# Seven block products for eight in three quarters of an MLP down-projection, with the block sums on GpSimd

## The chip, the core and the metric

The kernel runs on one core of one Trainium2 chip. The metric is the device time of one execution in microseconds (us). Timed are whole executions; beside them one execution was recorded by the hardware profiler, and all durations of single instructions come from that one.

## What is computed

The reference is one decoder block on 512 tokens of width 1024, all in float32. Two token mixers (a state-space branch and a gated delta rule) run side by side, are merged by gates and projected by w_out; an MLP follows. Only the part behind the mixers is touched in earnest:

```
x = x + g1 * rmsnorm(merged @ w_out, norm_mix_post)
h = rmsnorm(x, norm_mlp_pre) * (1.0 + sc2) + sh2
y = square(relu(h @ w_mlp_up)) @ w_mlp_down
x = x + g2 * rmsnorm(y, norm_mlp_post)
```

h is 512 x 1024, w_mlp_up is 1024 x 4096, w_mlp_down is 4096 x 1024. The up-projection and the down-projection are of the same size.

## The kernel before

Matmuls take float32 operands in the type fp32r, which keeps fewer bits. To keep accuracy every operand is split in two: a high half (the value cast to fp32r) and a low half (the value less its high half). `mm3` (line 149) then makes three matmuls of a pair of tiles: high by high, low by high, high by low. A weight tile of 128 x 1024 goes through `dense_w` (line 140): SyncE issues its load into a tile `raw`, ScalarE casts it to `whi` (line 145), VectorE subtracts to get `wlo` (line 146). Each of the three tags has three buffers, so weight n can't be split before the matmuls of weight n-3 are done.

The mixers (up to about line 1237) run in an order written out by hand. Behind them the instructions of each engine are put in order by a planner of the framework at build time, which goes by the program's order as its priority and by planned durations; each engine then runs its own list strictly in that order. GpSimd (POOL in the profile), VectorE (DVE), ScalarE (ACT), TensorE (PE) and SyncE's DMA queue (SP) each have such a list.

After the mixers come the branch projections, then w_out with the norms (lines 1271 to 1356). `norms` adds the residual into the tiles `x1`, which stay in SBUF to the end of the kernel, as do the two rows `gates`. `up_part` (line 1289) starts the first three hidden blocks of the MLP early.

The MLP (lines 1359 to 1438) goes over four quarters q of the 4096 hidden channels. In a quarter, eight hidden blocks m of 128 channels are made: 24 matmuls of 512 columns (8 slices of the contraction by 3), then on ScalarE a ReLU (line 1375) and a square (line 1378), which is the high half at once, and on VectorE the exact square (line 1377) and the low half (line 1379). The block is kept as `act`, 128 channels x 512 tokens, in two halves. 16 buffers of `act` allow a quarter's blocks to be made beside the last quarter's use of theirs. Then follow two halves hf of the 1024 output columns. For each, four banks of PSUM (one for each 128 tokens) collect over four weight tiles kp, each of which holds two slices of 128 hidden channels by 512 columns. In `down` (line 1382) a weight tile serves 4 token blocks x 2 slices x 3 = 24 matmuls; a quarter has 8 weight tiles and 192 matmuls. The banks are then added to the sums `ya` (copied by ScalarE, line 1408, in the first quarter; added by VectorE, line 1410, in the next ones). The last quarter ends with the last norm, the gate and the residual (lines 1413 to 1438), whose GpSimd multiply (line 1416) is the only work that GpSimd has in the MLP before its last microseconds.

[...]

Of the kernel before, what the change touches and what calls it, by code (L numbers as in the profile page):

```python
# [116 lines left out]
def hybrid_block(ctx: ExitStack, tc: tile.TileContext, x, cols, drow, rows, w_ada, w_ch, w_z,  # L117
# [284 lines left out]
    tok1 = const.tile([P, NC, P], F32, name="tok1")  # L402
    tok2 = const.tile([P, NC, P], F32, name="tok2")
    neg = const.tile([P, NC, 16], F32, name="neg")
    elast = const.tile([P, H, NC], F32, name="elast")
# [10 lines left out]
    eye = const.tile([P, 8, 32], F32, name="eye")  # L416
# [854 lines left out]
    lp = ctx.enter_context(tc.tile_pool(name="lp", bufs=1))  # L1271
    gates = []
    for n in range(2):
        g = fin.tile([P, D], F32, name=f"gate{n}")
# [5 lines left out]
        gates.append(g)  # L1280
    x1, xn = [], []
    for t in range(NC):
        xx = fin.tile([P, D], F32, name=f"x1{t}")
        nc.sync.dma_start(out=xx, in_=x[t * P:(t + 1) * P, :])
        x1.append(xx)
# [17 lines left out]
    def norms(half):  # L1303
# [5 lines left out]
        for t in tt:  # L1309
            xx = lp.tile([P, D], F32, tag="act", name="xn", bufs=16)  # L1310
            for i in range(2):
                hs = slice(i * T, (i + 1) * T)
                ve.scalar_tensor_tensor(out=xx[:, hs], in0=pp[t, i], scalar=r1[:, t % 2:t % 2 + 1],  # L1313
                                        in1=gates[0][:, hs], op0=MUL, op1=MUL)
# [44 lines left out]
    ya = [lp.tile([P, D], F32, name=f"ya{t}") for t in range(NC)]  # L1359
    sq = [lp.tile([P, 1], F32, name=f"sqn{t}") for t in range(NC)]  # L1360
    for q in range(4):
        act = []
        for m in range(8):
            mm = q * 8 + m
            if mm < len(ups):
                ps = ups[mm][1]
            else:
                w = dense_w(w_mu[mm])
                ps = lpsum()
                for k in range(KD):  # L1370
                    ks = slice(k * P, (k + 1) * P)
                    mm3(ps, (w[0][:, ks], w[1][:, ks]), h2[k], k == 0, k == KD - 1)
            a = lp.tile([P, 2, T], F32R, tag="act", name="act", bufs=16)
            rl = lp.tile([P, T], F32, tag="rl", name="rl", bufs=2)
            sc.activation(rl, ps, AF.Relu)
            s = lp.tile([P, T], F32, tag="cv", name="sq", bufs=3)
            ve.scalar_tensor_tensor(out=s, in0=ps, scalar=0.0, in1=rl, op0=MAX, op1=MUL)
            sc.activation(a[:, 0, :], rl, AF.Square)
            ve.tensor_sub(out=a[:, 1, :], in0=s, in1=a[:, 0, :].bitcast(F32))
            act.append(a)  # L1380

        def down(ps, t, w, kp, a=0, b=T):
            ts = slice(t * P, (t + 1) * P)
            for k in range(2):
                kk = 2 * kp + k
                mm3(ps[:, a:b], (act[kk][:, 0, ts], act[kk][:, 1, ts]),
                    (w[0][:, k * T + a:k * T + b], w[1][:, k * T + a:k * T + b]), kk == 0, kk == 7)
        for hf in range(2):
            hs = slice(hf * T, (hf + 1) * T)
            end = q == 3 and hf == 1  # L1390
            pp = [lpsum() for _ in range(NC)]
            if end:
                extra = [lp.tile([P, 2, T], F32R, tag="act", name="wx", bufs=16).rearrange("p a b -> p (a b)")
                         for _ in range(2)]
                ws = [dense_w(w_md[q, hf, kp], extra if kp == 3 else None) for kp in range(4)]
                pp.append(lpsum())
                for n, (a, b) in enumerate(((0, T), (0, T), (0, T), (0, 256), (256, T))):
                    for kp in range(4):
                        down(pp[n], min(n, 3), ws[kp], kp, a, b)
            else:  # L1400
                for kp in range(4):
                    w = dense_w(w_md[q, hf, kp])
                    for t in range(NC):
                        down(pp[t], t, w, kp)
            for t in range(NC):
                y = ya[t][:, hs]
                if q == 0:
                    sc.copy(y, pp[t])
                elif not end:
                    ve.tensor_add(out=y, in0=pp[t], in1=y)  # L1410
                if q < 3:
                    continue
                if hf == 0:
                    sc.activation(junk[:, 0:T], y, AF.Square, accum_out=sq[t])  # L1414
                    ve.tensor_scalar(out=sq[t], in0=sq[t], scalar1=1.0 / D, scalar2=EPS, op0=MUL, op1=ADD)
                    gp.tensor_tensor(out=y, in0=y, in1=gates[1][:, hs], op=MUL)  # L1416
                    continue

                s1 = sq[t]
                for a, b in ((0, 256), (256, T)) if t == NC - 1 else ((0, T),):  # L1420
                    ve.tensor_add(out=y[:, a:b], in0=pp[t + (a > 0)][:, a:b], in1=y[:, a:b])
                    sh = lp.tile([P, 1], F32, tag="sh", name="sh", bufs=2)
                    sc.activation(junk[:, a:b], y[:, a:b], AF.Square, accum_out=sh)
                    sn = lp.tile([P, 1], F32, tag="s1", name="s1", bufs=2)
                    ve.scalar_tensor_tensor(out=sn, in0=sh, scalar=1.0 / D, in1=s1, op0=MUL, op1=ADD)
                    s1 = sn
                    if b == T:
                        gp.tensor_tensor(out=s1, in0=s1, in1=mhalf[:, 0:1], op=POW)
                    ve.tensor_mul(out=y[:, a:b], in0=y[:, a:b], in1=gates[1][:, T + a:T + b])
                ob = lp.tile([P, D], F32, tag="ob", name="ob", bufs=2)  # L1430
                for a, b in ((0, 256), (256, 640), (640, D)) if t == NC - 1 else ((0, T), (T, D)):
                    if b == 256:
                        sc.mul(ob[:, a:b], ya[t][:, a:b], s1)
                        gp.tensor_tensor(out=ob[:, a:b], in0=ob[:, a:b], in1=x1[t][:, a:b], op=ADD)
                    else:
                        ve.scalar_tensor_tensor(out=ob[:, a:b], in0=ya[t][:, a:b], scalar=s1, in1=x1[t][:, a:b],
                                                op0=MUL, op1=ADD)
# [87 lines left out]
```

## Time and profile before

| | |
|---|---|
| time, median of 3 runs | 1483.94 us (1483.15 to 1485.08) |
| the profiled execution's own time | 1484.77 us |
| its span, first to last instruction of the program | 1483.1 us |
| PE busy | 1458.1 us (98%), 8592 matmuls |
| DVE busy | 862.5 us (58%) |
| ACT busy | 732.6 us (49%) |
| POOL busy | 370.2 us (25%) |
| granted TensorE clock | 0.996 of full speed |

A row of the profile names the source line, the engine, the operation, the tile written and the tiles read, the shapes, and then times. A line can be that of a helper: all matmuls of `mm3` are on lines 150 to 152. Matmuls overlap in the pipeline, so the time of one is not its price in a stream: the price is the distance from one start to the next. Idle time stands in brackets behind an instruction, with what ended it. The granted clock is the share of its full clock that TensorE had.

### The profile page before, as it was taken

How to read it: one execution, taken by the hardware profiler on the slowest of the kernel's cores; microseconds unless marked ns; L12 is line 12 of the kernel's file. 1: busy time of each engine (PE TensorE's matmuls, PEld its weight loads, DVE VectorE, ACT ScalarE, POOL GpSimd, SP SyncE). 2: the span in 40 equal slices, each digit the busy share in tenths (PEclk: the TensorE clock that was granted, in tenths of full speed). 3: DMA queues.
4: the chain of work that ended last, by engine and by line, in shares of the span. 5: the costliest groups of instructions: out<-in, count | busy, mean ns of one | idle time of the engine just before them, and what ended most of it. 6: DMA issues, size and time to landing. Idle time of an engine off the chain costs nothing. (4 is left out here: it accounts for less than half of the span.)

```text
span 1483.1 us, 22692 instructions
## 1 busy us (share of the span) xinstructions
PE 1458.1 (98%) x8592; PEld 1241.0 (84%) x8592; DVE 862.5 (58%) x1522; ACT 732.6 (49%) x1379; POOL 370.2 (25%) x691
## 2 busy tenths in 40 slices
PE   9999999999999999999999899999999999999998
PEld 7788898879989889888888788888878888888886
DVE  3565577677767777676777634444477324343444
ACT  6575545673764747645665635333355333132232
POOL 3005444341814607336623410000011000000002
PEclk9999999999999999999999999999999999999999
DMA  9323434543434524344343449543372233223221
GB/s 360 127 97 118 150 103 125 128 137 97 151 119 138 158 81 151 121 116 138 116 137 119 158 170 331 175 156 127 110 239 88 97 100 100 89 96 99 93 95 69
DMA packets 87070, 199.47 MB, mean 134 GB/s; under 512 B 32504, under 2 KB 33024, under 8 KB 86960
## 3 DMA queue, kind: packets, MB, share of 16 engines
q1 hardware_dynamic: 86960, 198.01, 41.3%
q8 instruction: 68, 1.11, 0.3%
q14 instruction: 42, 0.34, 0.1%
HBM read 181.10 MB, written 16.88 MB: 133 GB/s over the span
## 5 line engine op out<-in xcount | busy, mean ns | idle before, releaser
L150 PE MATMUL ps<-hT,whi 128*128 128x512 f32 x688 | 285.7, 415 | 4.8 <-ACT whi L469 4.3
L151 PE MATMUL ps<-hT,wlo 128*128 128x512 f32 x688 | 269.8, 392 | 1.2 <-DVE wlo L471 1.2
L152 PE MATMUL ps<-hT,whi 128*128 128x512 f32 x688 | 269.9, 392 | 0.0
L146 DVE TENSOR_TENSOR wlo<-raw,whi 128x1024 fp32r<-128x1024 f32 x114 | 140.0, 1229 | 199.7 <-ACT whi L145 199.7
L145 ACT CAST whi<-raw 128x1024 fp32r<-128x1024 f32 x114 | 119.4, 1048 | 210.1 <-PE pl L151 61.9
L150 PE MATMUL ps<-whi,hT 128*128 128x256 f32 (+1 forms) x536 | 166.3, 310 | 2.2 <-ACT y L715 1.4
L471 DVE TENSOR_TENSOR wlo<-raw,whi 128x1024 fp32r<-128x1024 f32 x103 | 128.1, 1244 | 64.2 <-ACT whi L469 60.3
L150 PEld LDWEIGHTS ps<-hT,whi 128*128 128x128 f32 x688 | 129.9, 189 | 31.9 <-ACT whi L469 4.5
L152 PE MATMUL ps<-wlo,hT 128*128 128x256 f32 (+1 forms) x536 | 154.3, 288 | 0.6 <-DVE wlo L471 0.6
L151 PE MATMUL ps<-whi,hT 128*128 128x256 f32 (+1 forms) x536 | 153.8, 287 | 0.0
L152 PEld LDWEIGHTS ps<-hT,whi 128*128 128x128 f32 x688 | 129.7, 189 | 28.3
L151 PEld LDWEIGHTS ps<-hT,wlo 128*128 128x128 f32 x688 | 130.1, 189 | 25.8 <-DVE wlo L471 2.4
L469 ACT CAST whi<-raw 128x1024 fp32r<-128x1024 f32 x103 | 107.3, 1044 | 67.4 <-PE ps L152 47.1
L533 DVE SCALAR_TENSOR_TENSOR cv<-ps,col,cv 128x511 f32<-128x511 f32 (+1 forms) x180 | 133.0, 742 | 8.0 <-ACT cv L527 5.4
L150 PEld LDWEIGHTS ps<-whi,hT 128*128 128x128 f32 x536 | 102.1, 190 | 5.8 <-ACT y L715 1.6
L825 POOL TENSOR_TENSOR tm<-Ub,Nb 128x60 f32<-128x60 f32 (+24 forms) x248 | 93.7, 378 | 52.5 <-DMA Nb<-btd 37.6
L151 PEld LDWEIGHTS ps<-whi,hT 128*128 128x128 f32 x536 | 102.1, 190 | 2.2
L152 PEld LDWEIGHTS ps<-wlo,hT 128*128 128x128 f32 x536 | 101.8, 190 | 2.0 <-DVE wlo L471 0.8
L827 POOL TENSOR_TENSOR Ub<-Ub,tm 128x60 f32<-128x60 f32 (+24 forms) x248 | 95.0, 383 | 19.4
L1416 POOL TENSOR_TENSOR ya<-ya,gate 128x512 f32<-128x512 f32 x4 | 5.8, 1466 | 324.8 <-ACT junk L1414 324.8
L150 PE MATMUL pl<-hT,whi 128*128 128x512 f32 (+1 forms) x184 | 66.6, 363 | 1.0 <-DVE hT L195 1.0
L151 PE MATMUL pl<-hT,wlo 128*128 128x512 f32 (+1 forms) x184 | 66.1, 362 | 0.4 <-DVE wlo L146 0.4
(502 smaller groups left out, 3049.0 us busy)
## 6 DMA issues: line engine op xcount, KB each, us to landing
raw<-in_w_ch SPq DMA_DIRECT2D x81, 512.0 KB
raw<-in_w_ada SPq DMA_DIRECT2D x48, 512.0 KB
raw<-in_w_z SPq DMA_DIRECT2D x32, 512.0 KB
raw<-in_w_up SPq DMA_DIRECT2D x32, 512.0 KB
raw<-in_w_mu SPq DMA_DIRECT2D x32, 512.0 KB
raw<-in_w_md SPq DMA_DIRECT2D x32, 512.0 KB
dc<-acd SPq DMA_DIRECT2D x16, 512.0 KB
ydr<-y SPq DMA_DIRECT2D x32, 256.0 KB
```

The lines of the kernel that those rows point to most:

```text
L145: sc.copy(hi, raw)
L146: ve.tensor_sub(out=lo, in0=raw, in1=hi.bitcast(F32))
L150: pe.matmul(ps, lhsT=lhs[0], rhs=rhs[0], start=first, stop=False)
L151: pe.matmul(ps, lhsT=lhs[1], rhs=rhs[0], start=False, stop=False)
L152: pe.matmul(ps, lhsT=lhs[0], rhs=rhs[1], start=False, stop=last)
L469: sc.copy(hi, raw)
L471: ve.tensor_sub(out=lo, in0=raw, in1=hi.bitcast(F32))
L533: ve.scalar_tensor_tensor(out=t[:, s:], in0=ps[:, :T - s], scalar=col[:, o + k:o + k + 1], in1=t[:, s:], op0=MUL, op1=ADD)
L825: gp.tensor_tensor(out=t3, in0=Ub[:, 0:r, j:j + 1].to_broadcast([P, r, n]), in1=Nb[:, j:j + 1, j + 1:32].to_broadcast([P, r, n]), op=MUL)
L827: gp.tensor_tensor(out=Ub[:, 0:r, j + 1:32], in0=Ub[:, 0:r, j + 1:32], in1=t3, op=SUB)
L1416: gp.tensor_tensor(out=y, in0=y, in1=gates[1][:, hs], op=MUL)
```

## The change

In quarters 0 to 2 the down-projection is made by a scheme of seven block products (Strassen's, in Winograd's form). The tokens are halved (256 each), the output columns are halved (512 each) and the hidden slices are taken in pairs (k0, k1), so that each pair of hidden slices gives a two-by-two block product: four activation blocks of 128 x 256 and four weight blocks of 128 x 512. In place of eight block products, seven are made, of sums and differences of blocks. The function `down7` does a quarter:

- For each pair kp it loads both weight tiles of the pair (both column halves), forms two weight differences on GpSimd, makes two hidden blocks (`hidden`), squares them into one float32 tile `pr` of four blocks, and forms the activation sums on GpSimd.
- `unit` splits two activation blocks (128 x 512 in all, or one of 128 x 256) in high and low halves, `wide` does the same to weight blocks: the cast on ScalarE, the subtraction on VectorE or GpSimd, as the caller says.
- `stage` goes over the four pairs kp with one split weight tile, one split activation tile and one or two block products of two token blocks each (`product`: three matmuls of 512 columns). The first three stages make two of the seven products each, 48 matmuls in a stage, and the fourth makes one, 24 matmuls.
- The second stage's weight tile is, once it is split, overwritten by GpSimd with the two weight differences of the third stage.
- Banks that belong to more than one output block are added to `ya` and then go on collecting (`add`, and start=False).

Quarter 3 is computed as before. To make room, `x1` is written to DRAM in `norms` and read back before the last half, `gates[0]` lives in a pool that is closed before the MLP, some tiles of the mixers move to the mixers' own pool, and `act` has 8 buffers, shared with the units. The last quarter's tiles take the tags of those pools.

The core of the diff:

```
...
+            nc.sync.dma_start(out=x1d[t], in_=x1[t])
...
+    def halves(src, dst, en):
+        sc.copy(dst[0], src)
+        en.tensor_tensor(out=dst[1], in0=src, in1=dst[0].bitcast(F32), op=SUB)
+        return dst
+    def unit(src, n, en):
+        u = mp.tile([P, 2, n, 256], F32R, tag="act", name="unit", bufs=8)
+        return halves(src, (u[:, 0], u[:, 1]), en)
+    def wide(src, en=None):
+        n = src.shape[1]
+        return halves(src, [wp.tile([P, 2, T], F32R, tag=tag, name=tag)[:, 0:n] for tag in ("whi", "wlo")], en or ve)
+    def product(ps, u, ub, w, wb, tt, first, last):
+        ts = slice(tt * P, (tt + 1) * P)
+        for n, (i, j) in enumerate(((0, 0), (1, 0), (0, 1))):
+            pe.matmul(ps, lhsT=u[i][:, ub, ts], rhs=w[j][:, wb], start=first and n == 0, stop=last and n == 2,
+                      skip_group_check=True)
+    def down7(q):
+        raw, tb, pr, s12, u1 = {}, [], [], [], []
+        for kp in range(4):
+            for hf in range(2):
+                raw[hf, kp] = mp.tile([P, 2, T], F32, tag="wr", name="wr", bufs=8)
+                nc.sync.dma_start(out=raw[hf, kp].rearrange("p a b -> p (a b)"), in_=w_md[q, hf, kp])
+            b1, b2 = raw[0, kp], raw[1, kp]
+            t = mp.tile([P, 2, T], F32, tag="tt", name="tt", bufs=4)
+            gp.tensor_tensor(out=t[:, 0], in0=b2[:, 0], in1=b1[:, 0], op=SUB)
+            gp.tensor_tensor(out=t[:, 1], in0=b2[:, 1], in1=t[:, 0], op=SUB)
+            tb.append(t)
+            a = mp.tile([P, 4, 256], F32, tag="pr", name="pr", bufs=4)
+            for k in range(2):
+                _, rl = hidden(q * 8 + 2 * kp + k)
+                sc.activation(a[:, 2 * k:2 * k + 2].rearrange("p a b -> p (a b)"), rl, AF.Square)
+            pr.append(a)
+            sm = mp.tile([P, 2, 256], F32, tag="s12", name="s12", bufs=4)
+            gp.tensor_tensor(out=sm[:, 0], in0=a[:, 1], in1=a[:, 3], op=ADD)
+            gp.tensor_tensor(out=sm[:, 1], in0=sm[:, 0], in1=a[:, 0], op=SUB)
+            gp.tensor_tensor(out=a[:, 1], in0=a[:, 0], in1=a[:, 1], op=SUB)
+            s12.append(sm)
+            u1.append(unit(a[:, 0:4:2], 2, ve))
+            gp.tensor_tensor(out=a[:, 2], in0=a[:, 2], in1=sm[:, 1], op=SUB)
...
+        def stage(us, ws, plan, after=None):
+            for kp in range(4):
+                w = ws(kp)
+                u = us(kp)
+                for ps, ub, wb, start in plan if kp < 3 else plan[::-1] if len(plan) > 1 and after else plan:
+                    for tt in range(2):
+                        product(ps[tt], u, ub, w, wb, tt, start and kp == 0, kp == 3)
+        banks = lambda: [lpsum() for _ in range(2)]
+        pa, pc = banks(), banks()
+        stage(lambda kp: u1[kp], lambda kp: wide(raw[0, kp]), [(pa, 0, 0, True), (pc, 1, 1, True)])
+        for tt in range(2):
+            add(tt, 0, pa[tt], True)
+            add(tt, 0, pc[tt])
+        pb_ = banks()
+        def w2(kp):
+            w = wide(tb[kp])
+            gp.tensor_tensor(out=tb[kp][:, 0], in0=raw[0, kp][:, 1], in1=tb[kp][:, 1], op=SUB)
+            gp.tensor_tensor(out=tb[kp][:, 1], in0=raw[1, kp][:, 1], in1=raw[1, kp][:, 0], op=SUB)
+            return w
+        stage(lambda kp: unit(s12[kp], 2, ve), w2, [(pb_, 0, 0, True), (pa, 1, 1, False)], True)
+        for tt in range(2):
+            add(tt, 1, pa[tt], True)
+        for tt in range(2):
+            add(tt + 2, 1, pb_[tt], True)
+        pc = banks()
+        stage(lambda kp: unit(pr[kp][:, 1:4:2], 2, gp), lambda kp: wide(tb[kp]), [(pc, 1, 0, True), (pa, 0, 1, False)], True)
+        for tt in range(2):
+            add(tt + 2, 1, pa[tt])
+            add(tt + 2, 0, pa[tt], True)
+        for tt in range(2):
+            add(tt + 2, 0, pc[tt])
+        stage(lambda kp: unit(pr[kp][:, 2:3], 1, gp), lambda kp: wide(raw[1, kp][:, 1:2], gp), [(pb_, 0, 0, False)])
+        for tt in range(2):
+            add(tt, 1, pb_[tt])
...
+    x1 = [mp.tile([P, D], F32, tag="tt", name="x1r", bufs=4) for _ in range(NC)]
+    for t in range(NC):
+        nc.sync.dma_start(out=x1[t], in_=x1d[t])
...
```

More of the change, by code (lines that the diff above doesn't have):

```diff
@@ L401, in hybrid_block @@
     H = 48
[L402 to L405, printed above, removed]
+    tok1 = sp.tile([P, NC, P], F32, name="tok1", bufs=1)
+    tok2 = sp.tile([P, NC, P], F32, name="tok2", bufs=1)
+    neg = sp.tile([P, NC, 16], F32, name="neg", bufs=1)
+    elast = sp.tile([P, H, NC], F32, name="elast", bufs=1)
     nA = const.tile([H, 1], F32, name="nA")
@@ L415, in hybrid_block @@
         gp.memset(tl, 0.0)
-    eye = const.tile([P, 8, 32], F32, name="eye")
+    eye = sp.tile([P, 8, 32], F32, name="eye", bufs=1)
     gp.memset(eye, 0.0)
@@ L1268, in hybrid_block @@
     up.close()
[L1271 to L1274, printed above, removed]
+    x1d = dram.tile([NC, P, D], F32, name="x1d")
+    gate1 = fin.tile([P, D], F32, name="gate1")
+    norm_scope = ExitStack()
+    lp = norm_scope.enter_context(tc.tile_pool(name="lp", bufs=1))
+    gate0 = lp.tile([P, D], F32, name="gate0")
+    for n, g in enumerate((gate0, gate1)):
         nc.sync.dma_start(out=g, in_=adr[n].partition_broadcast(P))
@@ L1309, in norms @@
         for t in tt:
-            xx = lp.tile([P, D], F32, tag="act", name="xn", bufs=16)
+            xx = lp.tile([P, D], F32, tag="xn", name="xn", bufs=4)
             for i in range(2):
@@ L1356, in hybrid_block @@
             up_part(m, slice(half * 256, (half + 1) * 256))
[L1359 to L1366, printed above, removed]
-            else:
[L1368 to L1400, printed above, removed]
-                for kp in range(4):
[L1402 to L1437, printed above, removed]
-                    nc.sync.dma_start(out=out[t * P:(t + 1) * P, a:b], in_=ob[:, a:b])
@@ new lines, in hybrid_block, with hidden @@
+    norm_scope.close()
+    mp = ctx.enter_context(tc.tile_pool(name="mp", bufs=1))
+    ya = [mp.tile([P, D], F32, name=f"ya{t}") for t in range(NC)]
+    sq = [mp.tile([P, 1], F32, name=f"sqn{t}") for t in range(NC)]
+    def hidden(mm):
+        if mm < len(ups):
+            ps = ups[mm][1]
+        else:
+            w = dense_w(w_mu[mm])
+            ps = lpsum()
+            for k in range(KD):
+                ks = slice(k * P, (k + 1) * P)
+                mm3(ps, (w[0][:, ks], w[1][:, ks]), h2[k], k == 0, k == KD - 1)
+        rl = mp.tile([P, T], F32, tag="rl", name="rl", bufs=2)
+        sc.activation(rl, ps, AF.Relu)
+        return ps, rl
@@ new lines, in down7, with add @@
+    def down7(q):
[21 more added lines that the diff above has]
+            gp.tensor_tensor(out=a[:, 2], in0=a[:, 2], in1=sm[:, 1], op=SUB)
+        def add(tt, hf, ps, first=False):
+            y = ya[tt][:, hf * T:(hf + 1) * T]
+            if first and q == 0:
+                sc.copy(y, ps)
+            else:
+                ve.tensor_add(out=y, in0=ps, in1=y)
+        def stage(us, ws, plan, after=None):
[32 more added lines that the diff above has]
+            add(tt, 1, pb_[tt])
@@ new lines, in hybrid_block, with down @@
+    for q in range(3):
+        down7(q)
+    act = []
+    for m in range(8):
+        ps, rl = hidden(24 + m)
+        a = mp.tile([P, 2, T], F32R, tag="act", name="act", bufs=8)
+        s = mp.tile([P, T], F32, tag="pr", name="sq", bufs=4)
+        ve.scalar_tensor_tensor(out=s, in0=ps, scalar=0.0, in1=rl, op0=MAX, op1=MUL)
+        sc.activation(a[:, 0, :], rl, AF.Square)
+        ve.tensor_sub(out=a[:, 1, :], in0=s, in1=a[:, 0, :].bitcast(F32))
+        act.append(a)
+    def down(ps, t, w, kp, a=0, b=T):
+        ts = slice(t * P, (t + 1) * P)
+        for k in range(2):
+            kk = 2 * kp + k
+            mm3(ps[:, a:b], (act[kk][:, 0, ts], act[kk][:, 1, ts]),
+                (w[0][:, k * T + a:k * T + b], w[1][:, k * T + a:k * T + b]), kk == 0, kk == 7)
```

47 lines of the change are left out of this document (44 added, 3 removed).

## The prediction

> **What bounds the kernel now.** I read the page's busy times first, then two stretches of the MLP in the table of busy time by stretch, then PE's timeline inside a down-projection.
>
> ```profile
> PE 1458.1 (98%) x8592; PEld 1241.0 (84%) x8592; DVE 862.5 (58%) x1522; ACT 732.6 (49%) x1379; POOL 370.2 (25%) x691
> ```
>
> ```profile
> 1210.60:1254.80 44.20, 44.20 (x196) 36.57 (x195) 18.86 (x22) 15.98 (x23) 0.00 (x0) 1.00 0.29 95
> 1254.80:1299.40 44.60, 44.60 (x194) 36.15 (x193) 15.76 (x17) 9.57 (x11) 0.00 (x0) 1.00 0.29 96
> ```
>
> The two rows are quarter 1: eight hidden blocks, then 192 down matmuls. After start, end and length the columns are PE, PEld, DVE, ACT and POOL busy, the granted clock, and the DMA share. PE is busy for all of both stretches at full clock, DVE for 16 to 19 of 44 us, ACT for 10 to 16, POOL not at all, DMA at 29%. So only fewer matmuls can shorten the MLP, and each other engine has room, on average, for work that replaces them.
>
> ```profile
> 1166.47 0.40 PE L150 MATMUL pl<-whi,act 128*128 128x512 f32 x1
> ...
> 1175.31 0.39 PE L152 MATMUL pl<-wlo,act 128*128 128x512 f32 x1
> ```
>
> These are the 1st and the 39th matmul (13 triples) of quarter 0's down-projection: 8.84 us for 38 steps, 0.2326 us from start to start. That is the price of a matmul in a stream; the 0.39 of one row is its length in the pipeline.
>
> **What is removed.** A quarter's down-projection goes from 192 to 168 matmuls (48 + 48 + 48 + 24) of the same shape: 24 x 0.2326 = 5.58 us, and 16.7 us for three quarters. The seven-product stretch needs 168 x 0.2326 = 39.1 us of PE: its stages end at 11.2, 22.3, 33.5 and 39.1 us from its start. The MLP's up-projection and quarter 3 keep their matmuls.
>
> **What is added, by engine.** The prices:
>
> ```profile
> L145 ACT CAST whi<-raw 128x1024 fp32r<-128x1024 f32 x114 | 119.4, 1048 | 210.1 <-PE pl L151 61.9
> ```
>
> ```profile
> L1378 ACT ACTIVATE act<-rl x32: 628/629/641, 1136.2 to 1432.6; 128x512 fp32r<-128x512 f32 x32
> L146 DVE TENSOR_TENSOR wlo<-raw,whi x114: 1208/1226/1661, 865.0 to 1454.3; 128x1024 fp32r<-128x1024 f32 x114
> L1379 DVE TENSOR_TENSOR act<-sq,act x32: 684/685/686, 1137.5 to 1433.9; 128x512 fp32r<-128x512 f32 x32
> L1410 DVE TENSOR_TENSOR ya<-pl,ya x14: 681/688/692, 1273.6 to 1453.5; 128x512 f32<-128x512 f32 x14
> L1416 POOL TENSOR_TENSOR ya<-ya,gate x4: 1289/1380/1812, 1451.4 to 1456.8; 128x512 f32<-128x512 f32 x4
> L1156 POOL TENSOR_TENSOR xk<-xk,zs x32: 733/744/1721, 228.1 to 870.7; 128x256 f32<-128x256 f32 x32
> ```
>
> The first is a row of the page's groups (busy us, mean ns, then idle time before). In the others the three figures behind a count are least, median and greatest duration in ns. For POOL I take the least, 1.29 us for 512 columns and 0.73 for 256, as the time of one that waited for nothing.
>
> ACT, in the seven-product stretch: at most 12 full weight casts (12.6 us), 4 half ones and 12 unit casts at 0.63 or less (10.1), so about 23 of 39 us. It stays beside PE. Nothing is booked; were ACT late by one cast, that would be 1.05 us.
>
> DVE: 12 full weight subtractions (14.7 us) in place of 8, 4 unit ones for the second stage (2.7), and 16 additions from PSUM (11.0) in place of 8: 28.4 of 39.1 us. By itself it fits too.
>
> POOL, in a whole quarter: 24 operations on 512 columns (two weight differences before and two after the second stage's split, a unit's and a weight's low half, for each of 4 pairs) and 20 on 256 (four block sums and one unit's low half): 24 x 1.29 + 20 x 0.73 = 45.6 us; PE has for it the eight hidden blocks and the stretch:
>
> ```profile
> 1216.76 0.60 ACT L1375 ACTIVATE rl<-pl 128x512 f32<-128x512 f32 x1 [4.15 <-PE pl L152]
> ...
> 1254.84 0.60 ACT L1375 ACTIVATE rl<-ps 128x512 f32<-128x512 f32 x1 [3.38 <-PE ps L152]
> ```
>
> These are the first and the eighth ReLU of quarter 1, each set off by the last matmul of its hidden block: 38.08 us for 7 blocks, 5.44 us for one, 43.5 us for eight. With the 39.1 that is 82.6 us, so POOL fits as well. But POOL and DVE do not run beside each other freely:
>
> ```profile
> 1453.28 1.30 POOL L1416 TENSOR_TENSOR ya<-ya,gate 128x512 f32<-128x512 f32 x1 [0.40 <-ACT junk L1414]
> 1455.01 1.81 POOL L1416 TENSOR_TENSOR ya<-ya,gate 128x512 f32<-128x512 f32 x1 [0.42 <-ACT junk L1414]
> ```
>
> ```profile
> 1453.48 0.69 DVE L1410 TENSOR_TENSOR ya<-pl,ya 128x512 f32<-128x512 f32 x1
> 1454.34 1.32 DVE L146 TENSOR_TENSOR wlo<-raw,whi 128x1024 fp32r<-128x1024 f32 x1 [0.17 <-ACT whi L145]
> ```
>
> The addition from PSUM (L1410) ran inside the first POOL operation at its usual 0.69. The weight subtraction (L146, both inputs in SBUF) started 0.24 us before that POOL operation ended, at 1454.58, and ended at 1455.66, that is 1.08 after it. The second POOL operation started inside the subtraction and ended at 1456.82, 1.16 after it. So a POOL operation and a DVE subtraction with two SBUF inputs take turns; the one that waits then needs 0.13 to 0.15 us less than alone, as its start is already behind it. I call what they take turns at the shared port, and its holds 1.08 (weight, DVE) and 1.15 (512 columns, POOL), and by the same 0.14 less than alone 0.55 (unit, DVE) and 0.59 (256 columns, POOL). The second pair is an estimate from the rows above.
>
> [...]
>
> **The port's bill.** Over a quarter: DVE 20 x 1.08 + 8 x 0.55 = 26.0, POOL 24 x 1.15 + 20 x 0.59 = 39.4, together 65.4 of 82.6 us. It fits. Over the seven-product stretch it does not. A split weight can be made only when the weight three before it is done, so at the stretch's start two of its weights are ready and the third's buffer comes free just then. What must then pass the port before PE can go on with the next quarter:
>
> - DVE: ten weight subtractions (the third to the twelfth weight), 10.8; the last pair's two units, 1.1; the next quarter's first hidden weight, 1.1. Sum 13.0.
> - POOL: the last pair's four block sums, 2.4; eight weight differences, 9.2; the third stage's units, 4.6; the fourth stage's units, 2.4; its weights, 4.6; and the next quarter's first weight differences for two pairs, which can be queued between these, 4.6. Sum 27.8.
>
> 40.8 us of port, and the port has nothing of this until the last hidden block's ReLU and square are through, some 1.2 us (twice 0.6). 42.0 less 39.1 is 2.9; I book a stall of 3.0 us a quarter. Ends: without the next quarter's differences it is 37.4, under 39.1, so no stall; with full durations in place of the holds it is 8.6 (the second rival). I take the middle since the handover rows give the holds, and POOL would otherwise be idle when those differences come up. The stall should sit in the third and fourth stages: the first begins with two weights ready, each weight's buffer is free 5.6 us ahead, and the late ones are the third stage's last weights, which need POOL's differences first.
>
> **Waits that come with it.** A DVE subtraction that waits for POOL holds up what is queued behind it: additions from PSUM. Banks `pa` go on collecting after an addition, so PE waits for it at the second and third stage; the first six matmuls of these stages go to another bank (1.4 us), and the stage before them ends with the other product (1.4 us more): 2.8 us of cover for two additions, 1.4 us, and a wait of 1.15. Booked at nothing; uncovered it would be about 1 us a time.
>
> The hidden blocks lose the exact square and the low half on DVE (16 operations of about 0.69 a quarter) and gain POOL's sums and a unit; the first unit of the last pair is due 8.4 us after the last hidden matmul, and ReLU, square, three sums, cast and subtraction are 0.6 + 0.6 + 3 x 0.73 + 0.6 + 0.7 = 4.7. Nothing.
>
> `x1` to DRAM and back:
>
> ```profile
> GB/s 360 127 97 118 150 103 125 128 137 97 151 119 138 158 81 151 121 116 138 116 137 119 158 170 331 175 156 127 110 239 88 97 100 100 89 96 99 93 95 69
> 1105.49 20.02 SPq L142 DMA_DIRECT2D raw<-in_w_mu  x6
> ```
>
> At the best slice's 360 GB/s a tile of 0.52 MB is 1.5 us. The reads have all of quarter 3's hidden blocks to land, 43 us. The stores stand in SP's queue among the w_out and w_mu loads, and wait there for the residual's addition with loads behind them; those loads are issued many us ahead (the six at 1105.49 go out over 20 us). Between 0 and one tile's 1.5 us I take 0.5, nearer to nothing. The tiles moved between pools, quarter 3's eight `act` buffers (free before its first square, 5.4 us into its first block) and the end cost nothing; a conflict there would show as a PE wait of a us or so at 1134 or 1454.
>
> **The sum.** 1484.8 (the profiled execution) - 16.7 + 3 x 3.0 + 0.5 = 1477.6. That execution lies 0.8 above the median of the runs, so 1476.8 for a median.
>
> **Rivals.**
>
> *PE stays the bound.* POOL's work for the next quarter keeps out of the stretch, the port has 37.4 us of claims and PE 39.1. For it: over the quarter the port has 17 us to spare, and each claim may slip by several us until it is due. Against: 37.4 leaves room for hardly one turn lost. 1484.8 - 16.7 + 0.3 - 0.8 = 1467.6.
>
> *The port becomes the bound.* Place: the seven-product stretch, third and fourth stage. Price at durations of one that waits for nothing: DVE 11 x 1.23 + 2 x 0.69 = 14.9, POOL 20 x 1.29 + 8 x 0.73 = 31.6, with 1.2 of start 47.7 us against 39.1: 8.6 us a quarter, 3.0 more than the matmuls saved. 1484.8 - 16.7 + 25.8 + 0.5 - 0.8 = 1493.6. It decides from a stall of 5.58 us a quarter on. For it: in-order lists laid out without turns lose time between turns. Against: the handover rows are shorter than full durations. [...]
>
> *DVE's queue gives it all back.* In the second stage DVE has 4 weight subtractions (4.9), 4 additions (2.8) and up to 4 waits of 1.15: 12.3 against 11.2 us, and the same at the fourth, so 2.2 more a quarter: 1484.8 - 16.7 + 15.6 + 0.5 - 0.8 = 1483.4, no change. Against: two weights of lead.
>
> That the seven products need more matmuls than counted is excluded by the loops.
>
> **How the numbers follow.** A measurement of this kernel tells about 0.2%, 3 us, from no change. Forecast (stall of 1.5 to 4.5 us a quarter, 1472 to 1481): 0.45. PE the bound: 0.25. DVE's queue: 0.1. The port: 0.2. Faster is the first two, 0.7; the same 0.1; slower 0.2. The range for 8 in 10 goes from just under the PE case to a little over the no-change case: 1466.5 to 1488; it leaves out most of the port's case.
>
> **What would show it.** In the profile after: 72 matmuls fewer, PE at 0.2326 a step within the stages. PE idle time with DVE weight or unit subtractions (or POOL low halves) as releasers, in quarters 0 to 2 alone, near 9 us in sum; POOL operations on 512 columns from 1.29 up to 2.4 us, DVE's weight subtraction up to 2.4, the additions still 0.69. No PE idle time there would show the port's bill wrong; idle time behind loads, or in the hidden blocks, would show the place wrong. The prediction fails if stalls exceed 5 us a quarter.

## The result and the profile after

The changed kernel takes 1509.57 us (median of 4 runs, 1504.29 to 1512.37) against 1484.51 of the kernel before (4 runs, 1483.15 to 1485.6). The ratio is 1.0165, with an interval of 1.0135 to 1.0195. The change makes the kernel slower by some 25 us; the prediction was 1476.8, faster by 8, and the time lies outside its range. The profiled execution took 1508.65 us with a span of 1506.9, so 23.8 us more than the span before. The accounts below are made against these two spans.

The page's busy times and granted clock of the kernel after:

```profile
PE 1453.5 (96%) x8520; PEld 1231.7 (82%) x8520; DVE 906.2 (60%) x1534; ACT 774.9 (51%) x1451; POOL 543.9 (36%) x823
...
PEclk9999999999999999999999999999989989999999
```

There are 72 matmuls fewer, as counted, but PE is busy for only 4.6 us less, and in two of the 40 slices, those that begin at 1092 and at 1206 us, its clock reads 8 tenths instead of 9 or more. The table of busy time by stretch shows where. Here are the down-projections of quarters 0 and 2 before (that of quarter 1 stands in the prediction, 44.60 us), and those of quarters 0 to 2 after, in the columns told there:

```profile
1166.20:1210.60 44.40, 44.40 (x192) 36.00 (x192) 11.10 (x10) 13.42 (x17) 0.00 (x0) 1.00 0.30 100
...
1343.30:1388.00 44.70, 44.70 (x194) 36.26 (x193) 16.12 (x18) 9.72 (x11) 0.00 (x0) 1.00 0.29 95
```

```profile
1176.10:1228.60 52.50, 43.95 (x170) 33.58 (x169) 28.22 (x24) 25.82 (x40) 43.44 (x30) 0.92 0.22 74
1272.90:1324.60 51.70, 42.75 (x169) 33.00 (x168) 35.54 (x32) 21.93 (x32) 42.83 (x30) 0.94 0.22 77
1368.70:1411.10 42.40, 39.72 (x169) 31.40 (x168) 34.38 (x31) 21.79 (x31) 35.56 (x24) 1.00 0.15 50
```

The stretches hold 168 matmuls instead of 192, and yet the first two are 8.1 and 7.1 us longer than before; the third, which no seven-product quarter follows, is 2.3 us shorter. In sum they take 146.6 us where the kernel before takes 133.7, 12.9 us more. A second loss lies ahead of the MLP. The same matmul, one that waits 1.0 us for a transposed block and starts the last part of the early hidden blocks, in PE's timeline before and after:

```profile
1121.65 0.39 PE L150 MATMUL pl<-hT,whi 128*128 128x256 f32 x1 [0.99 <-DVE hT L195]
```

```profile
1131.26 0.39 PE L150 MATMUL pl<-hT,whi 128*128 128x256 f32 x1 [1.00 <-DVE hT L195]
```

It comes 9.6 us later. 12.9 and 9.6 are 22.5 of the 23.8 us; the other 1.3 lies in the hidden blocks (0.6) and in quarter 3 and the end (0.7), by the same table's stretches, and was not followed. The list of PE's waits from the w_out stage to the end of quarter 2 (waited for: us in total, times, longest) shows both places:

```profile
PE pl L1398 <- POOL wlo L1382: 11.1, 4, 3.3
PE pl L150 <- ACT whi L145: 7.4, 1, 7.4
PE pl L1398 <- DVE wlo L1382: 4.4, 5, 1.1
PE pl L1398 <- DVE ya L1432: 3.5, 2, 1.8
PE ps L1398 <- DVE wlo L1382: 1.2, 1, 1.2
```

Line 1398 is the matmul of the seven products, line 1382 the subtraction that makes a low half, on DVE or on POOL, and line 1432 the addition of a bank to `ya`. The largest row is POOL's low halves of weights, of which the fourth stage has four a quarter. The second is not in the seven products at all: a weight of w_out that is late once by 7.4 us. Around it the granted clock is at half:

```profile
1090.20:1100.40 10.20, 4.96 (x11) 3.48 (x12) 4.90 (x4) 3.42 (x4) 0.00 (x0) 0.50 0.73 265
```

PE works for 4.96 us of it, at half pace; that is some 2.3 us more (an estimate from PE's timeline: the 11 matmuls from 1095.40 to 1100.24 start 0.44 us apart in place of 0.2326), and with the 7.4 it makes up the 9.6. Two theories were formed from this, one for each place.

**Fourth stage: the order of POOL's list.** POOL's timeline at the end of quarter 0, and PE's beside it:

```profile
1208.93 1.30 POOL L1411 TENSOR_TENSOR tt<-wr 128x512 f32<-128x512 f32 x1
1210.31 2.15 POOL L1412 TENSOR_TENSOR tt<-wr,tt 128x512 f32<-128x512 f32 x1
...
1213.11 1.30 POOL L1411 TENSOR_TENSOR tt<-wr 128x512 f32<-128x512 f32 x1
1214.50 1.26 POOL L1412 TENSOR_TENSOR tt<-wr,tt 128x512 f32<-128x512 f32 x1
...
1216.40 3.75 POOL L1382 TENSOR_TENSOR wlo<-wr,whi 128x512 fp32r<-128x512 f32 x3
1223.84 1.61 POOL L1411 TENSOR_TENSOR tt<-wr 128x512 f32<-128x512 f32 x1 [3.69 <-DMA wr<-in_w_md]
1225.40 1.26 POOL L1382 TENSOR_TENSOR wlo<-wr,whi 128x512 fp32r<-128x512 f32 x1
```

```profile
1217.71 0.80 PE L1398 MATMUL pl<-wlo,unit 128*128 128x512 f32 x1 [3.27 <-POOL wlo L1382]
1218.30 1.05 PE L1398 MATMUL ps<-whi,unit 128*128 128x512 f32 x2
1219.16 0.63 PE L1398 MATMUL ps<-wlo,unit 128*128 128x512 f32 x1
...
1226.72 0.80 PE L1398 MATMUL pl<-wlo,unit 128*128 128x512 f32 x1 [2.02 <-POOL wlo L1382]
```

Lines 1411 and 1412 are the next quarter's weight differences. Those of two pairs (1.30 + 2.15 + 1.30 + 1.26 = 6.0 us) stand right ahead of this quarter's fourth-stage low halves, and PE waits 3.27 us for the first of them. Then the third pair's difference finds no weight: POOL stands still for 3.69 us with the last low half queued behind it, and PE waits 2.02 us for that. SP's list of waits between 1195 and 1230 us says why the weight is late:

```profile
SPq L1408 <- POOL wlo L1382: 19.0, 4, 11.3
```

The load waits for the very low halves that POOL makes in this stage, since they are the last readers of its buffer.

The clock drops here too. Behind the first gap PE starts two matmuls in the 0.86 us from 1218.30 to 1219.16, 0.43 each where a stream has 0.2326, and the table has the granted clock:

```profile
1216.50:1223.30 6.80, 5.59 (x13) 4.43 (x14) 0.22 (x1) 1.66 (x2) 3.64 (x3) 0.50 0.57 185
```

It is at 0.50 here, behind a gap of 3.27 us; the last section has a gap of 1.75 us with 0.50 behind it. But between the two gaps the slow pace costs nothing. What sets the time there is POOL's last low half; by the rows above POOL waits for the load alone, and the load for POOL. A faster PE would only have waited longer than 2.02 us.

**Ahead of the MLP: late loads.** SP's timeline of DMA issues at w_out, before and after:

```profile
911.39 0.90 SPq L1275 DMA_DIRECT2D gate<-adr  x2
914.73 1.35 SPq L1284 DMA_DIRECT2D x<-in_x  x2
...
1075.95 3.01 SPq L142 DMA_DIRECT2D raw<-in_w_out  x2
```

```profile
1074.55 0.33 SPq L1277 DMA_DIRECT2D gate<-adr  x1
...
1084.54 0.91 SPq L1285 DMA_DIRECT2D x<-in_x  x2
1085.49 1.97 SPq L142 DMA_DIRECT2D raw<-in_w_out  x3
```

Before, the gate rows and the four tiles of x were loaded from 911 us on, long ahead. After, `gate0` and the tiles of x go out from 1074 to 1085 us, among the loads of w_out in SP's in-order list, and the w_out load that went out at 1075.95 before goes out at 1085.49. The theory: `gate0` and the `x1` tiles now lie in the pool `lp`, whose memory the branch projections hold until then, so that a load that used to be early must be late. The rival: it is only the place of these loads in the list that is at fault.

### The profile page after: what moved, and what is told of

Read it like the earlier page. It is cut to its first block, busy times and chain, and to the rows that moved or that the text cites. A ratio compares the mean times of both kernels' runs of the same rounds, so it can differ in the third digit from the quotient of the medians.

```text
span 1506.9 us, 22822 instructions
## 1 busy us (share of the span) xinstructions
PE 1453.5 (96%) x8520; PEld 1231.7 (82%) x8520; DVE 906.2 (60%) x1534; ACT 774.9 (51%) x1451; POOL 543.9 (36%) x823
## 5 line engine op out<-in xcount | busy, mean ns | idle before, releaser
L146 DVE TENSOR_TENSOR wlo<-raw,whi 128x1024 fp32r<-128x1024 f32 x90 | 111.7, 1243 | 179.0 <-ACT whi L145 177.8
L471 DVE TENSOR_TENSOR wlo<-raw,whi 128x1024 fp32r<-128x1024 f32 x103 | 128.8, 1251 | 64.0 <-ACT whi L469 62.6
L145 ACT CAST whi<-raw 128x1024 fp32r<-128x1024 f32 x90 | 94.3, 1048 | 135.4 <-PE pl L152 43.7
L469 ACT CAST whi<-raw 128x1024 fp32r<-128x1024 f32 x103 | 107.3, 1044 | 68.9 <-PE ps L152 48.6
L1398 PE MATMUL pl<-whi,unit 128*128 128x512 f32 x240 | 77.1, 403 | 3.5 <-DVE ya L1432 3.5
L784 POOL TENSOR_SCALAR_AFFINE_SELECT dec<-dec 128x1024 f32<-128x1024 f32 x8 | 9.0, 1122 | 165.2 <-DVE dec L779 136.7
```

The source lines that it names most:

```text
L145: sc.copy(hi, raw)
L146: ve.tensor_sub(out=lo, in0=raw, in1=hi.bitcast(F32))
L469: sc.copy(hi, raw)
L471: ve.tensor_sub(out=lo, in0=raw, in1=hi.bitcast(F32))
L1398: pe.matmul(ps, lhsT=u[i][:, ub, ts], rhs=w[j][:, wb], start=first and n == 0, stop=last and n == 2, skip_group_check=True)
```

## The experiments

The first four kernels ran beside a kernel before of 1485.36 us, the next four beside one of 1484.23, and the last two beside one of 1484.31.

### 1. The x and gate loads put behind later w_out loads

```
-            bb = lp.tile([P, D], F32, tag="ob", name="rb", bufs=2)
+            bb = lp.tile([P, D], F32, tag="ob", name="rb", bufs=4)
...
-            nc.sync.dma_start(out=x1d[t], in_=x1[t])
...
                 w = dense_w(w_out[hf, kp])
+                at = 8 * half + 4 * hf + kp
+                if at in (7, 9):
+                    n = at == 9
+                    with tc.issue_after(load[0].ins):
+                        gate_row(n, (gate0, gate1)[n])
+                        x_row(2 * n)
+                        x_row(2 * n + 1)
...
+    for t in range(NC):
+        nc.sync.dma_start(out=x1d[t], in_=x1[t])
     norm_scope.close()
```

`load[0]` is the last w_out load, `gate_row` and `x_row` load a gate row and a tile of x.

> The changed kernel with one edit ahead of the MLP: the loads of the gate rows and of x go out behind the eighth and the tenth w_out weight, with four buffers in place of two for the rows, and the stores of x1 stand at the end of the norms. Theory (SP's list): in the changed kernel these loads stand ahead of the eighth w_out load, and PE waits 7.5 us for it near 1095; without that the MLP's first hidden matmul comes 9 to 10 us earlier, near 1122 in place of 1131, the three seven-product stretches keep their 52.5, 51.7 and 42.4 us, and the time falls from about 1509 to 1499.5. Rival (the traffic itself, 4 MB more of stores and loads, or the memory that x must wait for): the wait comes back at another weight and less than 3 us are won.

Measured: 1507.65 us (1504.57 to 1510.16), ratio 1.0151 (1.0133 to 1.017), no different from the kernel after. PE's timeline has the reason; under it are the first of the same transposes in the kernel before:

```profile
1101.04 0.87 PE L194 MATMUL pl<-ident,xn 128*128 128x128 f32 x3 [5.89 <-issue]
```

```profile
1110.64 1.03 PE L192 MATMUL pl<-ident,xn 128*128 128x128 f32 x8
```

The 7.4 us wait for w_out is gone, so the place of these loads in SP's list does count. But PE now waits 5.89 us at the norm's transposes. The reason is not that x or the gates come too late: DVE begins the norm at 1093.03 and has its first block ready at 1100.94, where the kernel before begins at 1094.91 and has it at 1102.84. It is that the transposes now stand 60 matmuls earlier in PE's list, ahead of w_out matmuls that come first in the kernels before and after: the planner made a new order for PE as well. Why it did is open. So the experiment is a miss as a cure, and it decides nothing between the theory and the rival. Moving the stores of `x1` to the end of the norms did not show. The four fourth-stage waits stayed (11.0 us in sum).

### 2. All of the next quarter's differences behind the fourth stage

```
...
+        prev = low[0]
...
+            with tc.issue_after(prev.ins) if prev is not None and kp in (0, 1, 2, 3) else ExitStack():
+                gp.tensor_tensor(out=t[:, 0], in0=b2[:, 0], in1=b1[:, 0], op=SUB)
+                gp.tensor_tensor(out=t[:, 1], in0=b2[:, 1], in1=t[:, 0], op=SUB)
```

`low[0]` is the last low half of a weight that GpSimd has made.

> The changed kernel with one edit: on GpSimd the next quarter's first weight differences (8 operations) stand behind the last low half of the fourth stage, by an order edge without a wait. Theory (place in GpSimd's list): in quarters 0 and 1 these differences, and a wait for the next quarter's weights, stand ahead of low halves that PE waits for; behind them the stretches of quarters 0 and 1 come down to quarter 2's 42.4 us, the fourth stage's waits go, the granted clock stays at 1.00, and the time falls by 18 to 20 us to about 1490. Rival (the port's bill as a whole): the same claims only move, and come up again in the next quarter's hidden blocks or its second stage; the time falls by less than 10 us.

Measured: 1488.56 us (1487.08 to 1492.42), ratio 1.0026 (1.0017 to 1.0036), 0.0139 under the kernel after, or 20.6 us. The table by stretch, and POOL's timeline at the end of quarter 0:

```profile
1176.20:1218.90 42.70, 39.99 (x170) 31.19 (x168) 27.12 (x22) 25.70 (x40) 38.07 (x26) 1.00 0.26 87
1262.50:1304.90 42.40, 39.72 (x169) 31.41 (x168) 34.36 (x30) 21.80 (x31) 37.70 (x26) 1.00 0.27 86
1348.60:1392.50 43.90, 41.22 (x169) 32.54 (x168) 32.99 (x31) 21.79 (x31) 35.66 (x24) 0.96 0.15 48
```

```profile
1211.34 5.33 POOL L1384 TENSOR_TENSOR wlo<-wr,whi 128x512 fp32r<-128x512 f32 x4
1216.63 3.53 POOL L1417 TENSOR_TENSOR tt<-wr 128x512 f32<-128x512 f32 x2
```

The four low halves now run at once from 1211.34, ahead of the differences (line 1417 here), the first two stretches are 9.8 and 9.3 us shorter, and the fourth-stage waits are gone from PE's list. No work was taken away, only moved to another place: for these waits the order of POOL's list was the cause.

### 3. Only the third and fourth pair's differences behind it

The edit is that of experiment 2 with `kp in (2, 3)`.

> As e2_sums_after, but only pairs 2 and 3 of the next quarter's differences stand behind; those of pairs 0 and 1 keep their place ahead of the fourth stage's first low half. If the cost is GpSimd's time at that place (5 us of differences ahead of the first low half), the gap of 3.4 us at the fourth stage's first weight stays, and only the last pair's gap of 2.2 to 2.7 us and its slow clock go: 3 to 5 us a quarter, about 1501. If the cost is the wait for the next quarter's weights alone, nearly all of e2's gain comes with this.

Measured: 1499.15 us (1497.56 to 1500.1), ratio 1.0097 (1.008 to 1.0114). The stretches of quarters 0 and 1:

```profile
1174.20:1222.40 48.20, 41.61 (x170) 32.15 (x170) 27.70 (x23) 25.69 (x40) 41.55 (x29) 0.96 0.24 79
1265.90:1314.00 48.10, 41.68 (x169) 32.46 (x168) 34.98 (x31) 21.80 (x31) 41.35 (x29) 0.96 0.24 79
```

Against 52.5 and 51.7 us, the wait for the late weight, with the slow clock behind it, was worth 4.3 and 3.6 us. What is left above 42.7 and 42.4, 5.5 and 5.7 us, is POOL's time on the first two pairs, again with the slow clock behind its gap. So both parts of the theory show.

### 4. Experiments 1 and 2 together

> Both edits, of e1_loads_late and e2_sums_after. If the two causes are separate the gains add: 1509 less 9.5 less 19 is 1480.5, a few us below the kernel before (1484.5); what is left against 1467 is the 3.0 us a quarter at the second stage, where DVE's subtractions take turns with GpSimd. If they overlap, it stays above 1484.

Measured: 1488.33 us (1486.3 to 1491.16), ratio 1.0021 (1.001 to 1.0032), no different from experiment 2 alone. The transposes wait 5.9 us here too. So the second place was still open, and the next experiment takes what the theory named, the memory.

### 5. Experiment 2, and gate0 and x1 in memory of their own

```
+    x_scope = ExitStack()
+    xq = x_scope.enter_context(tc.tile_pool(name="xq", bufs=1))
...
-    gate0 = lp.tile([P, D], F32, name="gate0")
+    gate0 = xq.tile([P, D], F32, name="gate0")
...
-        xx = lp.tile([P, D], F32, name=f"x1{t}")
+        xx = xq.tile([P, D], F32, name=f"x1{t}")
...
     norm_scope.close()
+    x_scope.close()
```

The new pool opens ahead of the branch projections.

> e2_sums_after, and gate0 and the four x1 tiles in a pool of their own that opens ahead of the branch projections and closes ahead of the MLP, so that their loads need not wait for memory that the branch projections hold; rows and stores of x1 as in the changed kernel. Theory (memory): in the changed kernel these five loads wait for that memory and come out together with the w_out loads; placed early, PE's waits for w_out weights near 1085 to 1096 go, the first hidden matmul of the MLP is near 1122 and the time falls from e2's 1488.6 by 9 to 10 us, to about 1479. Rival (the order in SP's list or the stores): under 3 us are won.

Measured: 1479.54 us (1477.77 to 1482.12), ratio 0.9975 (0.9965 to 0.9985): 0.0051 under experiment 2, 7.6 us, and now faster than the kernel before. SP's timeline and PE's:

```profile
912.09 0.90 SPq L1279 DMA_DIRECT2D gate<-adr  x2
```

```profile
1121.30 0.39 PE L150 MATMUL pl<-hT,whi 128*128 128x256 f32 x1 [1.00 <-DVE hT L195]
```

The gate rows are loaded at 912 us again, x from 915 us on, and the matmul that came at 1131.26 comes at 1121.30, 0.35 ahead of the kernel before. The stores of `x1` still go to DRAM and come back. So the 9.6 us came from the memory that the moved tiles share, through loads that it made late, and not from the way through DRAM.

What is left here is a third loss: 42.7, 42.4 and 42.5 us in the stretches, 3.4 over the 39.1 of the matmuls. In the kernel after, quarter 2 shows it alone. DVE's timeline at the start of its second stage:

```profile
1374.44 5.78 DVE L1382 TENSOR_TENSOR unit<-s,unit 128x512 fp32r<-128x512 f32 x4
1380.14 1.21 DVE L1382 TENSOR_TENSOR wlo<-tt,whi 128x1024 fp32r<-128x1024 f32 x1
...
1381.88 1.93 DVE L1382 TENSOR_TENSOR wlo<-tt,whi 128x1024 fp32r<-128x1024 f32 x1
1383.73 1.27 DVE L1432 TENSOR_TENSOR ya<-pl,ya 128x512 f32<-128x512 f32 x2
1384.93 2.33 DVE L1382 TENSOR_TENSOR wlo<-tt,whi 128x1024 fp32r<-128x1024 f32 x1
```

Four units in a row take 1.45 us each instead of 0.69, since each takes turns with POOL, of which four operations run there without a break, from 1373.40 to 1379.66 us; behind them the stage's first weight is late, and the third addition waits behind a weight that takes 1.93. PE waits 0.9 us for the one and 1.8 for the other. The port, the prediction's name for what the two take turns at, is full here: by all rows of the two engines, from 1370.46, 1.8 us into the stretch, to 1408.93 there is always a POOL operation or a DVE operation with two SBUF inputs under way, but for holes of at most 0.14 us. The remaining experiments ask what makes the two waits: the order of these claims, or their number.

### 6. Experiment 5, with POOL's third-stage units held back

```
-            gp.tensor_tensor(out=tb[kp][:, 1], in0=raw[1, kp][:, 1], in1=raw[1, kp][:, 0], op=SUB)
+            diff.append(gp.tensor_tensor(out=tb[kp][:, 1], in0=raw[1, kp][:, 1], in1=raw[1, kp][:, 0], op=SUB))
...
+        def u3(kp):
+            with tc.issue_after(diff[0].ins) if kp in (0, 1, 2, 3) else ExitStack():
+                return unit(pr[kp][:, 1:4:2], 2, gp)
```

> e5_x_early, and on GpSimd the third stage's four unit low halves stand behind the first pair's two weight differences of the second stage (an order edge). In e2 each quarter keeps a stall of 3.0 us at the second stage's first weight and first added bank, while DVE's four second-stage unit subtractions take 1.45 us each in place of 0.69, with GpSimd's units between them. Theory (the port's turns): without those GpSimd units there, DVE's four take at most 1 us each, and both gaps (1.1 and 1.9 us) shrink to under half: 1.5 to 2.5 us a quarter, 1472 to 1475. Rival (DVE's own list: four units and two weights are too much at that place): the gaps stay within 0.5 us, 1478 to 1480.

Measured: 1479.3 us (1477.19 to 1480.29), ratio 0.9968 (0.9957 to 0.998), no different from experiment 5. All three stretches took 43.0 us. The 0.9 us wait for the first weight went, the wait for the addition shrank to at most 1.1, and in quarters 1 and 2 new waits of 0.6 to 0.8 us came up later in the stretch. A claim moved is a claim met elsewhere.

### 7. Experiment 5, with the second stage's units split as soon as their sums are there

```
-            s12.append(sm)
             u1.append(unit(a[:, 0:4:2], 2, ve))
+            s12.append(unit(sm, 2, ve))
...
-        stage(lambda kp: unit(s12[kp], 2, ve), w2, [(pb_, 0, 0, True), (pa, 1, 1, False)], True)
+        stage(lambda kp: s12[kp], w2, [(pb_, 0, 0, True), (pa, 1, 1, False)], True)
```

> e5_x_early, with the second stage's units split as soon as their sums are made, among the hidden blocks, in place of all four after the last pair's first unit; GpSimd's order unchanged. Theory (too much at one place): three of the four subtractions leave the stretch's start, DVE is 3 to 4 us ahead there, and the 3.0 us a quarter go nearly all: 1470 to 1472. Rival (GpSimd's long operations between DVE's): the weights still wait for GpSimd's units, and less than 1.5 us a quarter is won, over 1475.

Measured: 1475.85 us (1475.31 to 1476.97), ratio 0.9949 (0.9936 to 0.9962). DVE's units now lie among the hidden blocks, where by the prediction's bill the port has room (65.4 of 82.6 us over a quarter, an estimate):

```profile
1167.80:1208.70 40.90, 39.62 (x169) 31.50 (x168) 24.70 (x19) 24.22 (x36) 37.94 (x26) 1.00 0.28 89
```

That is quarter 0; the others take 41.0 and 40.9 us. Half of the 3.4 us is gone, with both waits at the second stage's start. What is left are waits of 0.5 to 0.7 us for weights in the third stage. One wait is new: 1.6 us in quarter 0's hidden blocks, for a weight's low half on DVE; it is in the four kernels with this edit and in none without it. ScalarE's timeline has the reason:

```profile
1152.85 0.62 ACT L1386 CAST unit<-s 128x512 fp32r<-128x512 f32 x1 [6.73 <-POOL s L1430]
```

The cast of the early unit now stands in ScalarE's list ahead of that weight's cast and waits 6.73 us for POOL's activation sum, which is made between and behind four weight differences in POOL's list (lines 1420 and 1421, from 1145.96 on). It is the fourth stage's pattern once more: an operation that is not due yet stands ahead of one that is.

### 8. Experiments 6 and 7 together

> Both edits, of e6_units_held and e8_s12_early. If they mend the same wait, the time is that of the better of the two, 1470 to 1472; with no stall at all in the three stretches the sum of the matmuls gives 1484.8 - 16.7 = 1468, and under that nothing of this change can go. GpSimd's units, held back, could be late for the third stage; then a gap shows there and the time is above e8's.

Measured: 1478.13 us (1474.81 to 1480.08), ratio 0.9961 (0.9947 to 0.9975), stretches of 41.3 us. Nothing is won over experiment 7; if the order counts here, it is not this one.

### 9. Experiment 7, with the third stage's units on DVE in place of POOL

```
-        stage(lambda kp: unit(pr[kp][:, 1:4:2], 2, gp), ...
+        stage(lambda kp: unit(pr[kp][:, 1:4:2], 2, ve), ...
```

> e8_s12_early, with the third stage's four unit low halves on DVE in place of GpSimd. Theory (the port's turns, GpSimd's long holds): one such operation holds the port 0.55 us on DVE and 1.15 on GpSimd, so 2.4 us of claims a quarter go, GpSimd's second differences come earlier, and the two gaps of 0.7 us at the third stage's last weights shrink: each stretch from 40.9 to 40.2 us or less, 1473 to 1474.5. Rival (DVE has no room: in the stretch it has 28 us of its own work and waits besides): its additions come late, new gaps at the added banks show, and the time is that of e8 (1475.9) or above.

Measured: 1473.37 us (1470.82 to 1477.66), ratio 0.9937 (0.9919 to 0.9956), the fastest kernel here that does all of the work, 10.9 us under the kernel before.

```profile
1167.80:1207.10 39.30, 39.30 (x170) 31.58 (x168) 30.30 (x23) 24.47 (x37) 33.24 (x22) 1.00 0.31 96
```

That is quarter 0; the others take 39.5 us each, and PE is busy for the whole of all three. DVE gained 4 subtractions a quarter and POOL lost them; POOL needs 1.29 us for one on its own (the least of L1416 in the kernel before) where DVE needs 0.69 (L1379), so by the prediction's estimate of the holds, 1.15 against 0.55, the port has less to do in all. The medians of this kernel and of experiment 7 are not told apart by their intervals; the stretches, 122.8 and 118.3 us in sum, are.

### 10. Experiment 7 without the second weight differences

```
-            gp.tensor_tensor(out=tb[kp][:, 0], in0=raw[0, kp][:, 1], in1=tb[kp][:, 1], op=SUB)
-            gp.tensor_tensor(out=tb[kp][:, 1], in0=raw[1, kp][:, 1], in1=raw[1, kp][:, 0], op=SUB)
```

The third stage uses the second stage's weights again. The kernel leaves out work that the result needs; its time only says what that work costs here.

> e8_s12_early without the two weight differences a pair that make the third stage's weights; the third stage then uses the second stage's weights again. GpSimd has 8 operations of 512 columns less in each stretch. Theory (GpSimd's work in the stretch, by turns and by its own time, is all that is left of the stall): no gap in the stretches, which fall from 40.9 to 39.1 to 39.5 us, and 5 to 6 us of the time, to 1470 to 1471. Rival (DVE and ACT alone limit the weights' splits at that pace): 40 us or more.

Measured: 1472.17 us (1469.18 to 1474.0), ratio 0.9917 (0.9897 to 0.9938), stretches of 39.0 to 39.3 us and no wait of PE in them. Taking 8 of POOL's operations a quarter off the port, or moving 4 to the cheaper engine, both clear the third stage; the one reordering that was tried did not. So what was left after experiment 7 goes with the amount of claims on the port at that place.

## Why the prediction was wrong

**What held.** The matmul's price in a stream and the 16.7 us for 72 of them: with the waits gone (experiment 9) the stretches take 118.3 us, 39.4 each against the 39.1 forecast, 15.4 us under the kernel before; with the 1.6 us wait of quarter 0's hidden blocks that leaves 13.8, and the span is 14.0 shorter (1469.1 against 1483.1). The turns at the port held too: POOL's 512-column operations ran from 1.26 up to 2.3 us, DVE's units in turns at 1.45, and DVE's weight of 1384.93 in quarter 2 (2.33 us, to 1387.26) ended 1.09 us behind the POOL operation it waited for, where the prediction had 1.08:

```profile
1384.89 1.28 POOL L1382 TENSOR_TENSOR unit<-pr,unit 128x512 fp32r<-128x512 f32 x1
```

The way of `x1` through DRAM cost nothing to be seen. And the prediction saw that the next quarter's first differences would come up inside the stretch.

**The step that failed first: a stall of 3.0 us a quarter.** PE's waits for the seven products sum to 20.2 us (11.1 + 4.4 + 3.5 + 1.2) where the prediction looked for 9, and the stretches took 146.6 - 3 x 39.1 = 29.3 us more than their matmuls, 9.8 a quarter, far beyond the 5.58 from which the sign turns. The bill added up what must pass the port by the stretch's end, and left out in which order POOL's list takes it and what an entry of the list waits for itself. Quarters 0 and 2 of the kernel after show the difference. The last low half on POOL is done at 1226.66 in quarter 0, 50.6 us after the stretch's start, and at 1408.94 in quarter 2, 40.2 us after it:

```profile
1403.61 5.33 POOL L1382 TENSOR_TENSOR wlo<-wr,whi 128x512 fp32r<-128x512 f32 x4
```

Of the 10.3 us between, 5.0 are the differences of two pairs, which the bill had at 4.6. The other 5.3 it didn't have: the third pair's difference (1.61 us) stands ahead of PE's last low half, its weight's buffer comes free only in the same stage, and POOL stands still for 3.69 us with PE's weight queued behind. No sum of claims contains such a wait. None of these operations is due before the next quarter's second stage. That their place in the list makes the loss is shown by experiments 2 and 3, which remove no operation and give back 20.6 and some 10 us. The rival "the port becomes the bound" had the sign, but not for its reason: it priced operations at full durations in place of the holds, and where the two engines take turns the holds were as the prediction had them (1.09 against 1.08 above). Only POOL operations that follow one another come near its 1.29: 1.33 us each in the row above.

**The second step: without the next quarter's differences no stall.** Quarter 2 of the kernel after is this case, and the bill gave 37.4 us of port against 39.1. It took 42.4, with the port full from 1.8 us after its start until POOL's last low half. The bill was too short for what stands at the start: it booked two units, the last pair's, but all four of the second stage's stand behind the last pair's first (the row of 5.78 us), so three more, 1.65 us by its own 0.55, come ahead of the second stage's first weight. That weight is late by 0.9 us, and then the additions from PSUM wait behind weights: the prediction booked these at nothing on 2.8 us of cover, which didn't last (1.8 us of PE's wait in quarters 1 and 2). The rival of DVE's queue named this mechanism, and priced it at 2.2 us a quarter on top of 3.0. Experiment 7, which takes units away from the start, won 1.5 to 1.8 us a quarter; experiments 9 and 10 show that the rest goes with the amount. What was left in between, waits for the third stage's weights, is the place that the prediction named.

**The third step: tiles moved between pools cost nothing.** They cost 9.6 us, the largest single term after the fourth stage. The prediction asked what the stores would hold up in SP's queue, and not when the moved tiles' memory comes free: with the end of the branch projections, so that the loads fall among those of w_out. Experiment 5, which gives them other memory, shows it. The prediction said that a conflict there would show at 1134 or 1454 us; it showed at 1095, in the stage ahead.

**A term that was missing altogether** is the clock behind a gap: some 2.3 of the 9.6 us at w_out. In quarters 0 and 1 it makes PE busy for 43.95 and 42.75 us in place of quarter 2's 39.72, but what falls between the two gaps is time in which PE would have waited. Behind the second gap it counts, and it reaches into the next hidden block, whose first matmuls, from 1228.59 on, still start 0.43 us apart.

Open are the 1.3 us outside both places, and why the planner moved the transposes in experiments 1 and 4.

## What to carry to other kernels

A sum of claims against the time that an engine or a port has says what fits, not what is on time. Go through the helper engine's list in its order, and ask of each item that is not due yet what stands behind it and what it waits for itself. When a tile is moved to another pool, ask when the memory below it comes free, since an early load can become a late one without any line of it changing (here `gate0`, from 911 to 1074 us). If an operation of two inputs in SBUF can go to either engine and the two take turns, the one that does it in half the time relieves both (here DVE with 0.69 us against POOL's 1.29: 4.5 us less in the three stretches of experiment 9 than of experiment 7).

## What the hardware showed

A gap of PE can cost more than its length, and not every time. The matmul behind the addition waited 1.76 us in quarter 1 of the kernel after and 1.75 in quarter 2 of experiment 2. PE's timelines, and under each the table's row for 3.4 us behind the gap:

```profile
1289.26 0.73 PE L1398 MATMUL pl<-whi,unit 128*128 128x512 f32 x2 [1.76 <-DVE ya L1432]
```

```profile
1289.30:1292.70 3.40, 3.40 (x15) 2.79 (x16) 3.40 (x3) 1.36 (x2) 3.32 (x3) 1.00 0.11 43
```

```profile
1365.00 0.74 PE L1402 MATMUL pl<-whi,unit 128*128 128x512 f32 x2 [1.75 <-DVE ya L1438]
```

```profile
1366.00:1369.40 3.40, 3.40 (x9) 2.63 (x8) 3.40 (x3) 1.13 (x2) 3.32 (x3) 0.50 0.00 0
```

Behind the first, PE goes on at full clock, with 15 matmuls in 3.4 us. Behind the second, from 1366.0 on, the granted clock is 0.50 and PE has 9. The stretch of the second is 43.9 us long where the same kernel's others have 42.4 and 42.7. So two gaps of the same length ended unlike; what decides it no run here shows.
